# Rotary part of a hybrid decoder layer: two head tiles share one inverse root, the rotation moves to VectorE

## The chip, the cores and the metric

The kernel runs on one core of one Trainium2 chip. The metric is the device time of one execution in microseconds, as the median of several runs.

## What is computed

One step of a decoder layer for a prompt of 512 positions and 32 sample positions (8 sequences of 4), 544 columns in all: a SwiGLU block, a mixing block, and a second SwiGLU block. The mixing block projects the normed input to q, k, v of eight attention heads and to q, k, v, o and gates of four mLSTM heads. The change touches the q and k of the attention heads:

```python
h = _rmsnorm(x, p['mix_norm'])
z = h @ w_in
aq = _rope(_rmsnorm(aq.reshape(B, T, N_ATT_HEADS, HEAD_DIM), q_gain), pos)
ak = _rope(_rmsnorm(ak.reshape(B, T, N_ATT_HEADS, HEAD_DIM), k_gain), pos)
...
x1, x2 = xf[..., :half], xf[..., half:]
return jnp.concatenate([x1 * cos - x2 * sin, x1 * sin + x2 * cos], axis=-1)
```

So each head of 64 numbers is divided by the root of its mean square, multiplied by a gain, and rotated by position. The norm of the whole input (`mix_norm`, the factor `rb` below) also ends in a number per column.

## The kernel before

Everything is kept transposed: features lie on the 128 partitions, the 544 columns (`N`) along a row, worked as two halves of 272 (`HN`). A weight matrix is cut into jobs of 128 output rows. `Raw` loads the weights (tile `wraw`), `Job.split` makes a rounded part `whi` on ScalarE and a rest `wlo` on VectorE, and `products` runs 48 matmuls per job (8 blocks of rows, three products, two halves) into a PSUM tile `mm`, of which there are two. The `after` of a job, a generator, empties that tile.

The mixing block's jobs are, in this order: the gates; q0 to q3; k0, k1, v0, v1; the four of mLSTM head 0; k2, k3, v2, v3; the mLSTM heads 1 to 3; then sixteen short jobs of `w_out`. `rope` is the `after` of the q and k jobs: tile j holds heads 2j and 2j+1. It multiplies the product by `rb` (`rz<-mm,rb`), squares it (`rs<-rz`, ScalarE), has SP's DMA queue swap the halves of each head into `rr`, sums the squares with a 128x128 matmul of ones (`aux<-rs,ca`), takes the inverse root in three ScalarE and three VectorE steps (`rsqrt`), rotates on GpSimd (`rz<-rz,cg`, `rr<-rr,sg`, `rz<-rz,rr`), and multiplies both (`rq<-rz,ry`). Tables `cg` and `sg` hold the gains with cosines and sines. `q_done`, `k_done` then transpose the tiles to rows for the outputs; `attention` begins with the products of q and k, `aux<-rq,rq`; `far_scores` multiplies cache rows with q on GpSimd (`pr<-kv,qb`), where q comes back by way of a DRAM tile `q_d`.

What sets the order is a planner inside the program, `Order`: each generator yields the time at which it can go on by the planner's own costs, and instructions are issued in that order. Each engine then runs its own list strictly in order, and SP's DMA queue does too. A change of one generator therefore moves everything after it in the same stage. All recorded instructions carry line 223 (other engines), 282 or 287 (TensorE).

`wo(m, last)` takes the products of `w_out`: eight jobs with the mLSTM heads 0 to 2 (three blocks of rows), then eight with mLSTM head 3 and the four attention tiles (five blocks), in the order 7, 0, 1, 2, 3 of `mixed`.

Of the kernel before, what the change touches and what calls it, by code (L numbers as in the profile page):

```python
# [8 lines left out]
F32 = mybir.dt.float32  # L9
F32R = mybir.dt.float32r  # L10
AF = mybir.ActivationFunctionType
OP = mybir.AluOpType
# [4 lines left out]
P = 128  # L17
D = 1024
S = 512
B = 8  # L20
T = 4
NS = B * T
N = S + NS
HN = N // 2
# [7 lines left out]
HD = 64  # L32
ROW = NH * HD
NM = 4
EPS = 1e-6
# [3 lines left out]
NK = P + T  # L39
# [12 lines left out]
class Order:  # L52
# [26 lines left out]
    def done(self, *tiles, kind="aux"):  # L79
        for p in tiles:  # L80
            self.free[kind].append(self.used[p.tensor.name][0] + 0.2)
# [58 lines left out]
    def R(self, *aps):  # L140
        return max(self.ready.get(a.tensor.name, (0.0, ""))[0] for a in aps) + 0.2
# [103 lines left out]
def hybrid_layer_kernel(ctx: ExitStack, tc: tile.TileContext, I: dict, C: dict, O: list):  # L245
# [8 lines left out]
    dram = ctx.enter_context(tc.tile_pool(name="scratch", bufs=1, space=DRAM))  # L254
    ctx.enter_context(tc.manual_schedule())

    od = Order()
    act, dve, pool = Engine(od, "act", nc.scalar), Engine(od, "dve", nc.vector), Engine(od, "pool", nc.gpsimd)
    dma = Engine(od, "dma", nc.sync)
    dma2 = pool  # L260
    R, U, done = od.R, od.U, od.done

    def halves(ap):
        return ap.rearrange("p (a b) -> p a b", a=2)
# [10 lines left out]
    def t2(name, shape=(P, N), dt=F32):  # L275
        return gp.tile(list(shape), dt, name=name, tag="t2", bufs=NT2)
# [4 lines left out]
    def mm(out, lhsT, rhs, start=True, stop=True, beside=False, **kw):  # L281
        nc.tensor.matmul(out, lhsT, rhs, start=start, stop=stop, **kw)  # L282
        n = size(rhs)
        od.issue("pe", 0.05 if beside else n / (2180.0 if rhs.dtype == F32R else 595.0), [out], [lhsT, rhs])
# [20 lines left out]
    epsc = small("epsc", (P, 1))  # L305
# [177 lines left out]
    def rsqrt(y, v, t):  # L483
        act.activation(t, v, AF.Ln)
        act.activation(y, t, AF.Exp, scale=-0.5)
        act.activation(t, y, AF.Square)
        yield R(t) - 0.3
        dve.tensor_tensor(t, t, v, op=OP.mult)
        dve.tensor_scalar(t, t, -0.5, 1.5, op0=OP.mult, op1=OP.add)
        dve.tensor_tensor(y, y, t, op=OP.mult)  # L490
# [351 lines left out]
    jobs = ffn_jobs("ffn1", lambda: n1, n2.add)  # L842
# [44 lines left out]
    rb = lambda: n2.rb  # L887
# [16 lines left out]
    for i, n in enumerate(("q_norm", "k_norm")):  # L904
        g = I[n]
# [20 lines left out]
    big = {}  # L926

    def masks_in():
        yield 0, 0, lambda: at[0] >= last_fast + 2
        a = wp.tile([P, 8, P], F32, name="ca", tag="wsp", bufs=8).rearrange("p k c -> p (k c)")  # L930
        b = wp.tile([P, 4 * P + NK + 2 * FAR * 32], F32, name="cb", tag="wsp", bufs=8)
        n = 0
        for t, names in ((a, (("maskA", S), ("bmask", 2 * NS), ("caus", P), ("ones64", P))), (b, (("maskR", 4 * P + NK),))):
            n = 0
            for name, w in names:
                big[name] = t[:, n:n + w]
                dma.dma_start(big[name], C[name])
                n += w
        big["sF"] = b[:, n:].rearrange("p (g i b h) -> p g i b h", g=2, i=FAR, b=4)
# [33 lines left out]

    qT, kT, vT, vR = [None] * 4, [None] * 4, [None] * 4, [None] * 4

    def rope(dst, j, i, last):
        def post(ps, full):
            yield 0, 0, lambda: rb() is not None
            z, r, sq = t2("rz"), t2("rr"), t2("rs")
            dve.tensor_tensor(halves(z), ps, halves(rb()), op=OP.mult)  # L980
            done(full, kind="mm")
            yield R(z) - 0.3
            act.activation(sq, z, AF.Square)
            yield R(z)
            for e in range(2):
                dma.dma_start(r[64 * e:64 * e + 32], z[64 * e + 32:64 * e + 64])
                dma.dma_start(r[64 * e + 32:64 * e + 64], z[64 * e:64 * e + 32])
            yield R(sq), 2
            v = t2("rv")
            mss = aux(), aux()  # L990
            for h, ms in enumerate(mss):
                mm(ms[:, :HN], big["ones64"], sq[:, h * HN:(h + 1) * HN])
                act.activation(v[:, h * HN:(h + 1) * HN], ms[:, :HN], AF.Identity, bias=epsc)
            done(*mss)
            yield R(r) - 0.3, 0, lambda: i in tabs
            z2 = t2("rz2")
            pool.tensor_tensor(z2, z, tabs[i][0], op=OP.mult)
            pool.tensor_tensor(r, r, tabs[i][1], op=OP.mult)
            pool.tensor_tensor(z2, z2, r, op=OP.add)
            z = z2  # L1000
            y = t2("ry")
            yield R(v) - 0.5
            yield from rsqrt(y, v, sq)
            yield R(z) - 0.3
            q = t2("rq")
            dve.tensor_tensor(q, z, y, op=OP.mult)
            dst[j] = q
            if j % 2 and last:
                od.spawn(last(j // 2), 2, R(dst[j]))
        return post  # L1010

    def plain(dst, j, last):
        def post(ps, full):
# [666 lines left out]
    def pair_jobs(c0, afters):  # L1680
        r = Raw(w_in, 0, 8, [c0, c0 + P])
        return [Job(r, i, mxs, a) for i, a in enumerate(afters)]

    def q_jobs(g):
        return pair_jobs(256 * g, [rope(qT, 2 * g + i, 0, q_done) for i in range(2)])

    def kv_jobs(g):
        return (pair_jobs(512 + 256 * g, [rope(kT, 2 * g + i, 1, k_done) for i in range(2)])
                + pair_jobs(1024 + 256 * g, [plain(vT, 2 * g + i, v_done) for i in range(2)]))

    def ml_jobs(h):
# [12 lines left out]
    def wo(m, last):  # L1704
        def post(ps, full):
            yield 0, 0, lambda: xT[m] is not None
            x = xT[m]
            dve.tensor_tensor(halves(x), ps, halves(x), op=OP.add)
            done(full, kind="mm")
            if last:  # L1710
                yield from n3.add(m)
            yield 0
        return post
# [2 lines left out]
        r = Raw(w_out, 4 * P, 3, [m * P, (m + 1) * P])  # L1716
        jobs += [Job(r, i, lambda k: mixed[4 + k], wo(m + i, False)) for i in range(2)]
    for m in range(0, KD, 2):
        r = Raw(w_out, 7 * P, 1, [m * P, (m + 1) * P], (0, 4))
        jobs += [Job(r, i, lambda k: mixed[(7, 0, 1, 2, 3)[k]], wo(m + i, True)) for i in range(2)]  # L1720

    yp = y_prompt[0].rearrange("(b p) d -> p b d", p=P)
    ysm = y_sample.flatten_outer_dims()
# [29 lines left out]
def constants():  # L1753
    import numpy as np

    f = np.float32
    c = {"ident": np.eye(P, dtype=f)}
    half = HD // 2
    inv = (10000.0 ** (-np.arange(half) / half)).astype(f)
    pos = np.concatenate([np.arange(S), PAST + np.tile(np.arange(T), B)]).astype(f)  # L1760
    ang = (pos[None, :] * inv[:, None]).astype(f).astype(np.float64)
    cs, sn = np.cos(ang).astype(f), np.sin(ang).astype(f)
    c["cos"] = np.concatenate([cs, cs, cs, cs], 0)
    c["sin"] = np.concatenate([-sn, sn, -sn, sn], 0)
    c["ones64"] = np.kron(np.eye(2), np.full((HD, HD), 1.0 / HD)).astype(f)
    a = np.arange(P)
    c["caus"] = np.where(a[:, None] <= a[None, :], 0.0, NEG).astype(f)
    s = np.arange(NS)
    ok = (s[:, None] // T == s[None, :] // T) & (s[:, None] <= s[None, :])
    c["causS"] = np.where(ok, 0.0, NEG).astype(f)  # L1770
    c["bmask"] = np.broadcast_to((s[None, :] // T % 2 == np.arange(2)[:, None]).astype(f).reshape(1, -1), (P, 2 * NS)).copy()
    mine = a % NS // T // 2 == a // NS
    c["own"] = ((a[:, None] % NS == s[None, :]) & mine[:, None]).astype(f)
    c["bm4"] = np.stack([mine & (a % NS // T % 2 == 0), mine & (a % NS // T % 2 == 1), ~mine], 1).astype(f)

    def bias(d, n):
        return np.where(n > 0, 8.0 * np.log(np.maximum(n, 1)), NEG).astype(f)

    d = 128 * (3 - np.arange(4))[None, :, None] + a[:, None, None] - a[None, None, :]
    n = ((d <= 128).astype(int) + (d % 4 == 0) + (d % 16 == 0)) * (d >= 0)  # L1780
    c["maskA"] = bias(d, n).reshape(P, S)
    c["hmask"] = (a[:, None] % NH == np.arange(NH)[None, :]).astype(f)
    c["sel"] = (a[:, None] // NH == np.arange(16)[None, :]).astype(f)
    i = a[:, None] // T + 32 * np.arange(3)[None, :]
    n2 = 1 + ((512 - 4 * i) % 16 == 0)
    bf = np.concatenate([bias(i, n2), np.zeros((P, 1), f)], 1)
    t = np.arange(T)[None, :]
    d = 128 + t - a[:, None]
    bn = bias(d, (1 + (d % 4 == 0) + (d % 16 == 0)) * (d <= 128))
    tt, uu = np.arange(T)[:, None], np.arange(T)[None, :]  # L1790
    bw = bias(tt, np.where(tt == uu, 3, np.where(uu < tt, 1, 0)))
    rt = a // NH % T
    far = np.where(rt[:, None, None] == a[None, None, :] % T, bf.T[None], NEG)
    c["maskR"] = np.concatenate([far.reshape(P, 4 * P), bn.T[rt], bw[rt]], 1).astype(f)
    c["brow"] = (a[:, None] // 32 == np.concatenate([np.arange(B), np.arange(B) - 4])[None, :]).astype(f)
    return c
# [35 lines left out]
```

## Time and profile before

| what | value |
|---|---|
| median of 3 runs | 1139.76 us (1139.7 to 1139.85) |
| the profiled execution, its own time | 1140.47 us |
| its span, first to last instruction | 1138.7 us |
| TensorE busy | 1110.7 us (98%) |
| VectorE busy | 783.9 us (69%) |
| ScalarE busy | 516.1 us (45%) |
| GpSimd busy | 155.5 us (14%) |
| mean granted TensorE clock | 0.996 |

The rows further down come from one execution, the profiled one, so sums are made against 1140.47 us. A bracket behind a row of a timeline is the time for which the engine was idle before that instruction, and what it waited for. TensorE's instructions overlap in the records: what one costs is read from start to start.

### The profile page before, as it was taken

The numbers are of one execution on the slowest core, as the hardware profiler recorded it, in microseconds if no ns is written. First come the engines' busy times: TensorE is split into PE (matmuls) and PEld (weight loads), VectorE is DVE, ScalarE is ACT, GpSimd is POOL, SyncE is SP. The second block draws the span as 40 slices with busy tenths as digits, with TensorE's granted clock in tenths as the row PEclk, the third lists the DMA queues.
The fourth block names the chain that finished last, engine by engine and source line by source line (L and its number), as shares of the span: only waits on it lengthen the run. The fifth ranks groups of instructions, "written<-read, shape, count | busy, mean of one in ns | idle before, by whom it ended". The sixth has DMA issues, their size and how long they took to land.

```text
span 1138.7 us, 21430 instructions
## 1 busy us (share of the span) xinstructions
PE 1110.7 (98%) x8819; PEld 1057.8 (93%) x8819; DVE 783.9 (69%) x1199; ACT 516.1 (45%) x926; POOL 155.5 (14%) x137
## 2 busy tenths in 40 slices
PE   7999999999999998999999999999999999999998
PEld 5989999999999998988877779999999999999998
DVE  5988337873487689889866546678972588537851
ACT  5545215451245455556653634463551345414541
POOL 0110000000000035467743201001100000000000
PEclk9999999999999998999999999999999999999999
DMA  7214412432143362685788644442233132422232
GB/s 229 75 40 131 132 38 75 141 119 76 37 139 107 115 212 68 191 276 172 239 268 281 205 128 136 126 149 75 75 112 104 28 128 75 149 75 74 66 104 59
DMA packets 141901, 143.12 MB, mean 126 GB/s; under 512 B 8453, under 2 KB 120485, under 8 KB 141805
## 3 DMA queue, kind: packets, MB, share of 16 engines
q1 hardware_dynamic: 141740, 141.76, 39.9%
q8 instruction: 69, 1.13, 0.4%
q14 instruction: 28, 0.22, 0.1%
q0 software_dynamic: 64, 0.00, 0.0%
HBM read 130.36 MB, written 9.15 MB: 123 GB/s over the span
## 4 chain that ended last, share of the span: by engine, by line
PE 79%; DVE 11%; DMA 3%; ACT 3%; issue 3%; POOL 1%; SPq 1%; ACTq 0%; DVEq 0%; POOLq 0%
PE mm L282 65%; PE aux L282 11%; DVE wlo L223 3%; PE aux L287 3%; ACT whi L223 2%; DMA kv<-in_cache_k_win_dram 2%; DVE ws L223 2%; DVE rs L223 1%; DVE wraw L223 1%; SPq L223 1%; DMA xt<-in_x_prompt_dram 1%; DVE cb L223 1%; DMA wraw<-in_ffn_w_up_dram 1%; DVE mo L223 0%; DVE bcum L223 0%
## 5 line engine op out<-in xcount | busy, mean ns | idle before, releaser
L223 ACT CAST whi<-wraw 128x1024 fp32r<-128x1024 f32 (+3 forms) x180 | 174.0, 986 | 122.7 <-PE mm L282 94.4
L223 DVE TENSOR_TENSOR wlo<-wraw,whi 128x1024 fp32r<-128x1024 f32 (+3 forms) x180 | 209.0, 1170 | 20.8 <-ACT whi L223 20.3
L282 PE MATMUL mm<-oh,wlo 128*128 128x272 f32 x720 | 209.3, 291 | 3.9 <-DVE wlo L223 3.8
L282 PE MATMUL mm<-oh,whi 128*128 128x272 f32 x720 | 207.4, 288 | 0.4 <-ACT whi L223 0.4
L282 PE MATMUL mm<-ol,whi 128*128 128x272 f32 x720 | 207.2, 288 | 0.0
L282 PE MATMUL mm<-xh,whi 128*128 128x272 f32 x720 | 160.7, 305 | 0.2 <-ACT whi L223 0.2
L282 PE MATMUL mm<-xh,wlo 128*128 128x272 f32 x720 | 150.1, 290 | 1.6 <-DVE wlo L223 1.6
L282 PE MATMUL mm<-xl,whi 128*128 128x272 f32 x720 | 150.3, 290 | 0.0
L282 PE MATMUL mm<-hh,whi 128*128 128x272 f32 x704 | 146.2, 289 | 0.0
L282 PE MATMUL mm<-hh,wlo 128*128 128x272 f32 x704 | 145.4, 288 | 0.0
L282 PE MATMUL mm<-hl,whi 128*128 128x272 f32 x704 | 145.4, 288 | 0.0
L223 DVE SCALAR_TENSOR_TENSOR x<-mm,x 128x544 f32<-128x544 f32 x48 | 34.8, 724 | 157.7 <-PE mm L282 157.7
L282 PEld LDWEIGHTS mm<-oh,wlo 128*128 128x128 f32 x720 | 135.4, 188 | 7.1 <-DVE wlo L223 5.9
L282 PEld LDWEIGHTS mm<-oh,whi 128*128 128x128 f32 x720 | 135.5, 188 | 0.7 <-ACT whi L223 0.6
L282 PEld LDWEIGHTS mm<-ol,whi 128*128 128x128 f32 x720 | 135.6, 188 | 0.0
L282 PEld LDWEIGHTS mm<-xh,whi 128*128 128x128 f32 x720 | 113.8, 191 | 12.8 <-issue 10.7
L282 PEld LDWEIGHTS mm<-xh,wlo 128*128 128x128 f32 x720 | 114.2, 190 | 2.0 <-DVE wlo L223 2.0
L282 PEld LDWEIGHTS mm<-xl,whi 128*128 128x128 f32 x720 | 114.3, 190 | 0.1
L282 PEld LDWEIGHTS mm<-hl,whi 128*128 128x128 f32 x704 | 110.4, 188 | 0.0
L282 PEld LDWEIGHTS mm<-hh,wlo 128*128 128x128 f32 x704 | 110.4, 188 | 0.0
L282 PEld LDWEIGHTS mm<-hh,whi 128*128 128x128 f32 x704 | 110.2, 188 | 0.1
L223 ACT CAST whi<-ws 128x1024 fp32r<-128x1024 f32 x54 | 56.7, 1050 | 106.3 <-DVE ws L223 106.2
(322 smaller groups left out, 1870.7 us busy)
## 6 DMA issues: line engine op xcount, KB each, us to landing
wraw<-in_ffn_w_gate_dram SPq DMA_DIRECT2D x40, 512.0 KB
wraw<-in_ffn_w_up_dram SPq DMA_DIRECT2D x36, 512.0 KB
wraw<-in_ffn_w_down_dram SPq DMA_DIRECT2D x16, 1024.0 KB
kv<-in_cache_k_win_dram SPq DMA_DIRECT2D x56, 256.0 KB
kv<-in_cache_v_win_dram SPq DMA_DIRECT2D x56, 256.0 KB
wraw<-in_w_in_dram SPq DMA_DIRECT2D x16, 512.0 KB
wraw<-in_ffn_w_down_dram SPq DMA_DIRECT2D x8, 768.0 KB
wraw<-in_w_in_dram SPq DMA_DIRECT2D x6, 1024.0 KB
```

The costliest lines, as they stand in the source:

```text
L223: r = fn(*args, **kw)
L282: nc.tensor.matmul(out, lhsT, rhs, start=start, stop=stop, **kw)
L287: nc.tensor.transpose(out, in_, idn)
```

## The change

`rope` now serves a pair of tiles. Each half reads the raw product from PSUM twice: ScalarE copies it (`rz`) for the swap and the square, VectorE multiplies it by the cosine table; VectorE also multiplies the swapped copy by the sines and adds. The factor `rb` is no longer multiplied in there. A further generator, `scales`, takes the sums of squares of both tiles with four matmuls whose weights are 32 columns wide, at two column positions, so that the four heads' sums land on rows 0, 1, 32 and 33 of one tile; multiplies them by the square of `rb`; takes one inverse root of 64 rows for both tiles; multiplies by `rb`; writes the four rows to a DRAM tile `y_d` and reads each back onto 64 partitions; and multiplies the rotated tiles by it. The `w_out` jobs take mLSTM head 3 last instead of first.

```diff
+    y_d = dram.tile([4, 4, N], F32, name="y_d")
+    rb2 = []
+
+    def rope(dst, g, i, last):
+        zs, sqs = [None] * 2, [None] * 2
+
+        def scales():
             yield 0, 0, lambda: rb() is not None
-            z, r, sq = t2("rz"), t2("rr"), t2("rs")
-            dve.tensor_tensor(halves(z), ps, halves(rb()), op=OP.mult)
-            done(full, kind="mm")
-            yield R(z) - 0.3
-            act.activation(sq, z, AF.Square)
-            yield R(z)
-            for e in range(2):
-                dma.dma_start(r[64 * e:64 * e + 32], z[64 * e + 32:64 * e + 64])
-                dma.dma_start(r[64 * e + 32:64 * e + 64], z[64 * e:64 * e + 32])
-            yield R(sq), 2
-            v = t2("rv")
+            if not rb2:
+                rb2.append(t2("rb2", (64, N)))
+                act.activation(rb2[0], rb()[0:64], AF.Square)
+            yield R(rb2[0], *sqs) - 0.2, 2
+            v, y, t = t2("rv", (64, N)), t2("ry", (64, N)), t2("rw", (64, N))
             mss = aux(), aux()
             for h, ms in enumerate(mss):
-                mm(ms[:, :HN], big["ones64"], sq[:, h * HN:(h + 1) * HN])
-                act.activation(v[:, h * HN:(h + 1) * HN], ms[:, :HN], AF.Identity, bias=epsc)
+                h_ = slice(h * HN, (h + 1) * HN)
+                for e in range(2):
+                    mm(ms[32 * e:32 * e + 32, :HN], big["ones"], sqs[e][:, h_], beside=e > 0, tile_position=(0, 32 * e))
+                dve.tensor_tensor(v[:, h_], ms[0:64, :HN], rb2[0][:, h_], op=OP.mult)
             done(*mss)
-            yield R(r) - 0.3, 0, lambda: i in tabs
-            z2 = t2("rz2")
-            pool.tensor_tensor(z2, z, tabs[i][0], op=OP.mult)
-            pool.tensor_tensor(r, r, tabs[i][1], op=OP.mult)
-            pool.tensor_tensor(z2, z2, r, op=OP.add)
-            z = z2
-            y = t2("ry")
-            yield R(v) - 0.5
-            yield from rsqrt(y, v, sq)
-            yield R(z) - 0.3
-            q = t2("rq")
-            dve.tensor_tensor(q, z, y, op=OP.mult)
-            dst[j] = q
-            if j % 2 and last:
-                od.spawn(last(j // 2), 2, R(dst[j]))
-        return post
+            yield R(v) - 0.3
+            act.activation(t, v, AF.Ln, bias=epsc[0:64])
+            act.activation(y, t, AF.Exp, scale=-0.5)
+            act.activation(t, y, AF.Square)
+            yield R(y) - 0.3
+            dve.tensor_tensor(y, y, rb()[0:64], op=OP.mult)
+            yield R(t) - 0.3
+            dve.scalar_tensor_tensor(t, v, EPS, t, op0=OP.add, op1=OP.mult)
+            dve.tensor_scalar(t, t, -0.5, 1.5, op0=OP.mult, op1=OP.add)
+            dve.tensor_tensor(y, y, t, op=OP.mult)
+            yield R(y)
+            n = 2 * i + g
+            for e in range(2):
+                dma.dma_start(y_d[n, 2 * e:2 * e + 2], y[32 * e:32 * e + 2])
+            ys = t2("rs"), t2("rs")
+            for e in range(2):
+                for d in range(2):
+                    dma.dma_start(ys[e][64 * d:64 * d + 64], sub(y_d, (4 * n + 2 * e + d) * N, [[0, 64], [1, N]]))
+            for e in range(2):
+                yield R(zs[e], ys[e]) - 0.3
+                q = t2("rq")
+                dve.tensor_tensor(q, zs[e], ys[e], op=OP.mult)
+                dst[2 * g + e] = q
+            od.spawn(last(g), 2, R(*dst[2 * g:2 * g + 2]))
+
+        def half(e):
+            def post(ps, full):
+                yield 0, 0, lambda: i in tabs
+                raw, r, z, sq = t2("rz"), t2("rr"), t2("rz2"), t2("rs")
+                act.copy(halves(raw), ps)
+                dve.tensor_tensor(halves(z), ps, halves(tabs[i][0]), op=OP.mult)
+                done(full, kind="mm")
+                yield R(raw)
+                for d in range(2):
+                    dma.dma_start(r[64 * d:64 * d + 32], raw[64 * d + 32:64 * d + 64])
+                    dma.dma_start(r[64 * d + 32:64 * d + 64], raw[64 * d:64 * d + 32])
+                act.activation(sq, raw, AF.Square)
+                sqs[e] = sq
+                if e:
+                    od.spawn(scales(), 0)
+                yield R(r, z) - 0.3
+                dve.tensor_tensor(r, r, tabs[i][1], op=OP.mult)
+                dve.tensor_tensor(z, z, r, op=OP.add)
+                zs[e] = z
+            return post
...
-        r = Raw(w_out, 7 * P, 1, [m * P, (m + 1) * P], (0, 4))
-        jobs += [Job(r, i, lambda k: mixed[(7, 0, 1, 2, 3)[k]], wo(m + i, True)) for i in range(2)]
+        r = Raw(w_out, 0, 4, [m * P, (m + 1) * P], (7 * P, 1))
+        jobs += [Job(r, i, lambda k: mixed[(0, 1, 2, 3, 7)[k]], wo(m + i, True)) for i in range(2)]
```

The constant `ones64` (128x128) becomes `ones` (128x32, two columns of 1/64 on one head's rows each), and `q_jobs`, `kv_jobs` call `rope` once per pair.

Three places where the lists of instructions move. VectorE before, around the step of the gates that forms `u`; the rows ahead of it are the inverse root of one q tile (`rs`, `ry`), the first reading of the next product (`rz<-mm,rb`) and the rest part of a weight job (`wlo`):

```order
L223 TENSOR_TENSOR wlo<-wraw,whi 128x1024
L223 TENSOR_TENSOR rs<-rs,rv 128x544
L223 TENSOR_SCALAR rs<-rs 128x544
L223 TENSOR_TENSOR ry<-ry,rs 128x544
L223 TENSOR_TENSOR rz<-mm,rb 128x544
L223 TENSOR_TENSOR wlo<-wraw,whi 128x1024
L223 TENSOR_TENSOR u<-bcum,mrow 4x544
```

VectorE of the change at the same step; `rv` is the sums of squares times the square of `rb`, and `rz_4870<-mm,cg` the first reading of a product:

```order
L223 TENSOR_TENSOR wlo<-wraw,whi 128x1024
L223 TENSOR_TENSOR rv<-aux,rb_4632 64x272 x2
L223 TENSOR_TENSOR rz_4870<-mm,cg 128x544
L223 TENSOR_TENSOR wlo<-wraw,whi 128x1024
L223 TENSOR_TENSOR u<-bcum,mrow 4x544
```

The three steps of an inverse root no longer stand between the split of weights and the reading of the product there.

VectorE of the change behind the sums of squares of k0 and k1 (first row), down to the first maxima of the attention (`pS,smax`):

```order
L223 TENSOR_TENSOR rv<-aux,rb_4632 64x272 x2
L223 TENSOR_TENSOR rr<-rr,sg 128x544
L223 TENSOR_TENSOR rz_4870<-rz_4870,rr 128x544
L223 TENSOR_TENSOR wlo<-wraw,whi 128x1024
L223 TENSOR_TENSOR ry<-ry,rb 64x544
L223 TENSOR_TENSOR rr<-rr,sg 128x544
L223 TENSOR_TENSOR rz_4952<-rz_4952,rr 128x544
L223 SCALAR_TENSOR_TENSOR rw<-rv,rw 64x544
L223 TENSOR_SCALAR rw<-rw 64x544
L223 TENSOR_TENSOR ry<-ry,rw 64x544
...
L223 TENSOR_TENSOR rq<-rz_4870,rs 128x544
L223 TENSOR_TENSOR rq<-rz_4952,rs 128x544
```

Ten steps lead to the row `ry<-ry,rw` that goes to DRAM; the two last rows need what comes back (left out between them: v1's reading, two weight splits, the two `rq` of q2 and q3, three steps of mLSTM head 0). Before, each tile's `rq` followed its own root directly.

SP's queue of the change at the same place:

```order
L223 DMA q_d<-qs 32x256
L223 DMA wraw<-in_w_in_dram 128x8x256
L223 DMA y_d<-ry 2x544 x2
L223 DMA rs<-y_d 64x544 x4
L223 DMA out_dram<-vr 128x256 x2
L223 DMA q_d<-qs 32x256
```

Before, the queue held no `y_d` and no `rs<-y_d`; six of them per pair are new, and what follows waits behind them. On TensorE the sums of squares of k0 and k1 stand 126 weight-job matmuls ahead of the first `aux<-rq,rq`, and those of k2 and k3 144 ahead of the transposes of the next mLSTM k tile, whose VectorE reading stands behind the `rq` of k3.

## Rows read from the trace of the kernel before

**Rows 1.** The page, part 1: busy time, share of the span, instructions

```profile
PE 1110.7 (98%) x8819; PEld 1057.8 (93%) x8819; DVE 783.9 (69%) x1199; ACT 516.1 (45%) x926; POOL 155.5 (14%) x137
```

**Rows 2.** Waits of TensorE: who waited for whom, us in total, times, longest

```profile
PE aux L282 <- ACT rs L223: 3.4, 1, 3.4
PE aux L282 <- ACT hN L223: 1.7, 1, 1.7
...
PE aux L287 <- DVE rq L223: 1.0, 1, 1.0
PE aux L287 <- DVE smax L223: 1.0, 1, 1.0
PE mm L282 <- DVE ml L223: 1.0, 1, 1.0
```

**Rows 3.** Timeline of TensorE from 438 to 458: start, duration, instruction, idle before

```profile
440.69 1.08 PE L282 MATMUL aux<-rs,ca 128*128 128x272 f32 x4
441.40 0.61 PE L282 MATMUL mm<-xh,whi 128*128 128x272 f32 x2
441.85 0.41 PE L282 MATMUL mm<-xl,whi 128*128 128x272 f32 x2
...
448.94 2.18 PE L282 MATMUL aux<-rs,ca 128*128 128x272 f32 x4 [3.41 <-ACT rs L223]
450.53 1.04 PE L282 MATMUL mm<-xh,whi 128*128 128x272 f32 x2
...
454.54 0.41 PE L282 MATMUL mm<-xh,wlo 128*128 128x272 f32 x2
```

**Rows 4.** Timeline of VectorE, 427 to 460

```profile
433.67 0.69 DVE L223 TENSOR_TENSOR rs<-rs,rv 128x544 f32<-128x544 f32 x1
434.39 0.44 DVE L223 TENSOR_SCALAR rs<-rs 128x544 f32<-128x544 f32 x1
...
440.59 3.69 DVE L223 TENSOR_TENSOR rs<-rs,rv 128x544 f32<-128x544 f32 x1
444.31 1.48 DVE L223 TENSOR_SCALAR rs<-rs 128x544 f32<-128x544 f32 x1
445.83 1.73 DVE L223 TENSOR_TENSOR ry<-ry,rs 128x544 f32<-128x544 f32 x1
447.48 0.71 DVE L223 TENSOR_TENSOR rz<-mm,rb 128x544 f32<-128x544 f32 x1
```

**Rows 5.** Timeline of GpSimd, 427 to 460

```profile
441.02 1.36 POOL L223 TENSOR_TENSOR rz<-rz,cg 128x544 f32<-128x544 f32 x1
442.34 1.35 POOL L223 TENSOR_TENSOR rr<-rr,sg 128x544 f32<-128x544 f32 x1
```

**Rows 6.** Windows: PE, PEld, DVE, ACT, POOL busy (instructions), granted clock, DMA share, GB/s

```profile
200.00:300.00 100.00, 100.00 (x798) 99.77 (x797) 60.44 (x73) 35.95 (x51) 0.00 (x0) 1.00 0.33 106
...
450.00:452.00 2.00, 2.00 (x8) 1.76 (x7) 2.00 (x2) 1.33 (x3) 2.00 (x2) 0.50 0.00 0
```

**Rows 7.** Timeline of TensorE, 645.8 to 648: four side by side, at 32 columns each

```profile
646.42 1.06 PE L282 MATMUL aux<-kv,pTA 128*32 128x512 f32 x8
647.42 0.44 PE L282 MATMUL aux<-pT,vr 128*64 128x128 f32 x4
```

**Rows 8.** Timeline of VectorE, 456 to 545

```profile
538.42 1.81 DVE L223 TENSOR_TENSOR rs<-rs,rv 128x544 f32<-128x544 f32 x1
540.27 2.38 DVE L223 TENSOR_SCALAR rs<-rs 128x544 f32<-128x544 f32 x1
```

**Rows 9.** Timeline of VectorE, 400 to 420: a PSUM reading of one half

```profile
407.70 0.44 DVE L223 SCALAR_TENSOR_TENSOR nt<-aux,nt 128x272 f32<-128x272 f32 x1
```

**Rows 10.** Timelines of SP's queue, 465 to 473, and of GpSimd, 460 to 480

```profile
466.71 0.52 SPq L223 DMA_DIRECT2D q_d<-qs  x1
467.28 0.41 SPq L223 DMA_DIRECT2D kv<-in_cache_k_win_dram  x1
471.80 0.62 SPq L223 DMA_DIRECT2D qb<-q_d  x1
...
475.10 3.78 POOL L223 TENSOR_TENSOR pr<-kv,qb 128x512 f32<-128x512 f32 x3 [10.06 <-DMA qb<-q_d]
```

**Rows 11.** Tile uw_d: duration min/median/max in ns, first and last start

```profile
L223 SPq DMA_DIRECT2D E<-uw_d x4: 332/376/848, 488.8 to 676.4; - x4
...
L223 SPq DMA_DIRECT2D uw_d<-u x1: 267/267/267, 451.6 to 451.6; - x1
```

More of the change, by code (lines that the diff above doesn't have):

```diff
@@ L932, in masks_in @@
         n = 0
-        for t, names in ((a, (("maskA", S), ("bmask", 2 * NS), ("caus", P), ("ones64", P))), (b, (("maskR", 4 * P + NK),))):
+        for t, names in ((a, (("maskA", S), ("bmask", 2 * NS), ("caus", P), ("ones", NS))), (b, (("maskR", 4 * P + NK),))):
             n = 0
@@ L974, in hybrid_layer_kernel @@
     qT, kT, vT, vR = [None] * 4, [None] * 4, [None] * 4, [None] * 4
-    def rope(dst, j, i, last):
-        def post(ps, full):
-            yield 0, 0, lambda: rb() is not None
-            z, r, sq = t2("rz"), t2("rr"), t2("rs")
-            dve.tensor_tensor(halves(z), ps, halves(rb()), op=OP.mult)
-            done(full, kind="mm")
-            yield R(z) - 0.3
-            act.activation(sq, z, AF.Square)
-            yield R(z)
-            for e in range(2):
-                dma.dma_start(r[64 * e:64 * e + 32], z[64 * e + 32:64 * e + 64])
-                dma.dma_start(r[64 * e + 32:64 * e + 64], z[64 * e:64 * e + 32])
-            yield R(sq), 2
-            v = t2("rv")
+    y_d = dram.tile([4, 4, N], F32, name="y_d")
@@ L1012, in plain @@
+        return [half(e) for e in range(2)]
     def plain(dst, j, last):
@@ L1684, in q_jobs @@
     def q_jobs(g):
-        return pair_jobs(256 * g, [rope(qT, 2 * g + i, 0, q_done) for i in range(2)])
+        return pair_jobs(256 * g, rope(qT, g, 0, q_done))
     def kv_jobs(g):
-        return (pair_jobs(512 + 256 * g, [rope(kT, 2 * g + i, 1, k_done) for i in range(2)])
+        return (pair_jobs(512 + 256 * g, rope(kT, g, 1, k_done))
                 + pair_jobs(1024 + 256 * g, [plain(vT, 2 * g + i, v_done) for i in range(2)]))
@@ L1764, in constants @@
     c["sin"] = np.concatenate([-sn, sn, -sn, sn], 0)
-    c["ones64"] = np.kron(np.eye(2), np.full((HD, HD), 1.0 / HD)).astype(f)
+    c["ones"] = np.pad(np.kron(np.eye(2), np.full((HD, 1), 1.0 / HD)), ((0, 0), (0, NS - 2))).astype(f)
     a = np.arange(P)
```

## The prediction

> **What bounds the kernel now.** I read the page's busy table first: TensorE is at work for 98% of the span [rows 1], so time can only come from work taken off TensorE or from its waits. The waits of TensorE, second, show which of them lie in the mixing stage, the only stage that the change reorders: 3.4 us for the squares of a rope tile, 1.7 for a mLSTM step, 1.0 for a finished k tile, 1.0 for a maximum of the attention, 1.0 for the last mLSTM head [rows 2], 8.1 us together. Third, TensorE's timeline around the longest [rows 3]: it stops for 3.41 us and starts again at 448.94. From there the granted clock is 0.50 [rows 6], the lower of the two levels (1.2 instead of 2.4 GHz), after a stop in which TensorE did nothing. The price is in the starts. A weight-job matmul takes 100/798 = 0.125 us at the full clock [rows 6], a pair 0.25. From 448.94 to 454.54 there are one group of ones-matmuls and 8 pairs: 5.60 us. At the full clock the group costs 441.85 - 440.69 - 0.25 = 0.91 us [rows 3], the 8 pairs 2.0. So the clock costs 5.60 - 2.91 = 2.7 us more, and this one stop 6.1 us.
>
> Fourth, why the squares were late. They need `rz<-mm,rb`, which VectorE began only at 447.48 [rows 4]. Three steps of the tile before stood ahead of it: 3.69, 1.48 and 1.73 us, where the same forms take 0.69, 0.44 and about 0.7 in a quiet stretch (the 0.69 and 0.44 are the first two rows of rows 4, the last is as the first). The quiet ones ran with GpSimd idle; the slow ones lie over GpSimd's rotation of a rope tile [rows 4, 5]. The excess is 5.1 us. So one engine off the path, GpSimd, held VectorE, VectorE held ScalarE, and ScalarE held TensorE.
>
> **The change part by part.** *Sums of squares.* Before: 8 tiles at 0.91 = 7.3 us of TensorE. After: 4 groups of four matmuls, two column positions at once. The lower bound on a group is two streams of 272 columns that share the array fully, 0.91; the upper is no sharing, 1.83. The nearest row is the four streams of 512 at 32 columns each, which take 1.00 from start to next start [rows 7], about the time of one such stream (0.455 x 512/272 = 0.86) with 0.14 for getting in and out. I take 2 x 0.455 + 0.14, and a little for the second way back: 1.1 us. Four groups cost 4.4, so 2.9 us of TensorE time go, all on the path. The Trainium skill (TensorEngine Tiling (Array Packing), Key Properties) says that a change of tiling mode drains TensorE, which speaks against eight such changes, and gives no price; its Theoretical Speedup table would allow twofold, a group of 0.91 and a saving of 3.7. The row's 1.00 instead of 0.86 agrees with a small drain, so I stay with 2.9.
>
> *Rotation off GpSimd.* 24 GpSimd instructions of at least 1.35 us [rows 5] go. GpSimd waits for other data in this stage in any case, once for 10 us [rows 10], so that is worth nothing by itself; it is worth what it held up. The 6.1 us stop goes: the reading of the next product no longer stands behind an inverse root there, and nothing on GpSimd overlaps. The 1.0 for the k tile and the 1.0 for the maximum stood behind the inverse root of k3, whose first two steps took 1.81 and 2.38 us under GpSimd [rows 8], 3.1 more than in quiet: these 2.0 us go too. The 1.7 and the last 1.0 belong to mLSTM heads and are kept.
>
> *VectorE's load.* Per tile it loses the scaling 0.71, 0.69 + 0.44 + 0.7 of the root and the product 0.7: 3.2 us. It gains a reading 0.71, two rotation steps and the product at 0.7, 2.8, and per pair two readings of half a tile at 0.44 [rows 9] and a root of 3 x 0.7 + 0.44: 3.4, half of it per tile. So +1.3 us a tile, +10 in all, beside TensorE. What hides it is the 6.0 us (48 x 0.125) of a job: a q or k job asks 4.5 + 1.2 (a weight split) = 5.7 us, to which the steps of the gates come. Summed in order from the first gate step at 409 to v1's reading, VectorE trails the end of the jobs by up to 2 us, against the 6 us until the PSUM tile is wanted again. If that cover went, the next job would stop for the rest. ScalarE loses about 1 us a tile: nothing.
>
> *DMAs.* Each pair adds two writes at about 0.27 and four reads at about 0.38 [rows 11] to SP: 2.1 us of issue, 8 for four pairs, and SP stops between them until the write has landed. Behind it stand swaps of the next tile, cache rows and weights. Weights are wanted two jobs (12 us) later, which covers that; `far_scores` starts later, and the order leaves its end some 200 weight-job matmuls ahead of the last jobs. The price of the way through DRAM is in the rows of `q_d`: written until 467.23, read back no earlier than 471.80, so 4.6 us; the reader started at 475.10, 2.7 us after the read was issued [rows 10]. So 0.5 + 4.6 + 1.5 + 2.7 = 9.3 us from root to use, where before there was none. The Trainium skill (DMA: Bandwidth & Descriptors, Anatomy of one DMA) puts the fixed part of a DMA at about 2.0 us, most of it the receipt; by that the way would take about 6.0, and the new waits below would vanish, 2.0 us less. The trace's 4.6 differs, and I go by the trace.
>
> *What is late next.* Place one: the first scores of the attention. From the sums of squares of k0 and k1 VectorE has 0.9 + 1.4 + 1.2 + 0.7 + 1.4 + 0.7 + 0.44 + 0.7 = 7.4 us of steps; with the group of 1.1, 9.3 through DRAM and the product 0.7 the first tile is ready after 18.5 us. TensorE has 1.1 + 126 x 0.125 = 16.9 us of work in between, plus transposes that I leave uncounted. So the wait is between 0 and 1.6. Place two: k2 and k3, whose products VectorE makes ahead of reading the next mLSTM k tile. There GpSimd multiplies cache rows all the time, so the steps can take up to 5 us more (as in the stretch of rows 8, four steps in place of 2.6): 23.5 and two products, against 1.1 + 18.0 us plus attention work of a few us. Wait between 0 and 4.4. Both together 0 to 6; I take 2.0, as the transposes and attention work left uncounted make both waits shorter.
>
> *Order of `w_out`.* mLSTM head 3 is used 24 matmuls (3.0 us) later; in the new order its transposes also stand 24 matmuls later. The 1.0 us wait stays: nothing. The attention pairs move later by up to 200 matmuls and still end 84 ahead of their use: nothing.
>
> **The sum**, against the profiled execution: 1140.47 - 2.9 - 6.1 - 2.0 + 2.0 = 1131.5 us. The median of the runs lies 0.7 below that execution, so 1130.8 for the median; with 0 to 6 for the new waits 1128.8 to 1134.8.
>
> **The rivals.** *Waits move, none go.* A new order finds new collisions of about the same size; only the 2.9 us of work go: 1140.47 - 2.9 - 0.7 = 1136.9, give or take 2. For it: VectorE is as full as before, and the stage holds a dozen chains planned to within a microsecond. Against it: the longest wait has a cause that is gone. *All waits go*, new ones don't come: 8.1 + 2.7 less as well, 1126.1. For it, GpSimd has little left to collide with; against it, the mLSTM waits have nothing to do with rope. *The way through DRAM decides, slower.* SP and VectorE run in order, so a late `y_d` blocks VectorE at `rq` and, behind it, the reading of PSUM tiles and weight splits. If TensorE then stops for as long as in rows 3 the clock falls with it, 6.1 us a pair. It decides from the point where the way through DRAM takes some 3.4 us more than the cover, that is from 13 instead of 9.3 us at place one. At two pairs it gives 1140.47 - 11.0 + 12.2 - 0.7 = 1141.0, at three 1147.1, at four 1153.2. For it, the measured 4.6; against it, q2 and q3 have far more cover than k. *The side-by-side matmuls don't overlap*: a group costs 1.83, nothing is saved there, 1133.7; rows 7 speak against it.
>
> **How the numbers follow.** A measurement of this kernel can tell some 0.2%, 2.3 us, from no change. Forecast 0.45, waits move 0.25, all go 0.10, slower through DRAM 0.15, no overlap 0.05. Faster by over 0.2% is below 1137.5: nearly all of the forecast (0.44), half of the second (0.12), 0.10 and 0.05: 0.71. Slower by over 0.2% is the third rival: 0.14. The rest, 0.15, is within. The range goes from 1125.5, under the case without waits, to 1141.5, where the DRAM case begins to bite.
>
> **What would show it.** Right: TensorE's wait for rope squares at about 445 gone and the granted clock 1.00 from 436 to 460; about 1.1 us for each of four groups `aux<-rs,ca` at 32 columns; no GpSimd on rope; VectorE's root steps at 0.4 to 0.7 us in the q jobs; SP waiting about 4 us for `y_d` per pair; a wait of TensorE of some 2 us for `rq` or behind it. Wrong: a stop of over 3 us with the clock at 0.50 after it; `y_d` landing in 2 us or in 8; waits elsewhere in the mixing stage that add up to 8 us again.

## The result and the profile after

The changed kernel takes **1130.34 us** (median of 4 runs, 1128.79 to 1133.5) beside 1139.73 for the kernel before (4 runs): a ratio of 0.9922, 95% interval 0.9901 to 0.9943. The forecast was 1130.8. Two later sets of 6 runs each gave 1131.62 and 1130.38. The profiled execution is the longest of its four: 1133.5 us, span 1131.7.

The busy table of the page [rows 1 before]:

```profile
PE 1106.0 (98%) x8819; PEld 1054.1 (93%) x8819; DVE 771.3 (68%) x1222; ACT 504.4 (45%) x900; POOL 112.0 (10%) x113
```

GpSimd is busy 43.5 us less, 42.0 of it the rotation. VectorE has 23 instructions more and is busy 12.6 us less.

To tell the mixing stage from the noise of the rest I measure it in each trace between two marks of TensorE that every version has: the squares of the norm ahead of it and of the norm behind it. The two marks in the timeline of the kernel before:

```profile
404.30 1.08 PE L282 MATMUL aux<-sq,onesd 128*128 128x272 f32 x4
...
756.65 1.08 PE L282 MATMUL aux<-sq,onesd 128*128 128x272 f32 x4
```

and of the changed kernel:

```profile
405.83 1.08 PE L282 MATMUL aux<-sq,onesd 128*128 128x272 f32 x4
...
749.70 1.08 PE L282 MATMUL aux<-sq,onesd 128*128 128x272 f32 x4
```

The stage went from 352.35 to 343.87 us, 8.5 less. The first mark alone moved by 1.5 us, in a part of the program that the change doesn't touch; so spans of single executions carry a noise of that size, and stages are better compared.

Waits of TensorE in the stage, 400 to 760, of the changed kernel (who waited for whom; total, times, longest) [rows 2 before]:

```profile
PE aux L287 <- DVE mk L223: 2.9, 1, 2.9
PE aux L282 <- ACT kt L223: 1.5, 2, 1.2
PE aux L287 <- DMA kv<-in_cache_k_win_dram: 1.0, 1, 1.0
PE aux L287 <- DVE C L223: 0.8, 1, 0.8
PE aux L282 <- DVE Cst L223: 0.3, 1, 0.3
```

Not one wait of before is left but that for a cache row (0.2 us before), and not one of the new ones is for rope. The stretch in which TensorE stopped before runs without a gap at the full clock (windows: busy, granted clock, DMA share) [rows 3, 6 before]:

```profile
445.00:450.00 5.00, 5.00 (x42) 1.00 0.76 221
450.00:455.00 5.00, 5.00 (x50) 1.00 0.38 111
```

The longest new wait, 2.9 us for an mLSTM k tile, looks like the old one: slowed steps of VectorE ahead of the one that TensorE wants. VectorE's timeline ahead of it:

```profile
590.77 1.77 DVE L223 TENSOR_TENSOR mo<-mo,ms 128x544 f32<-128x544 f32 x1
592.58 1.69 DVE L223 SCALAR_TENSOR_TENSOR mo<-mo,ms 128x544 f32<-128x544 f32 x1
594.19 1.86 DVE L223 TENSOR_REDUCE cb<-pr 128x8 f32<-128x512 f32 x3
595.97 0.71 DVE L223 SCALAR_TENSOR_TENSOR mk<-mm,rb 128x544 f32<-128x544 f32 x1
```

and GpSimd's, which multiplies cache rows for the sample scores at that moment:

```profile
590.67 3.02 POOL L223 TENSOR_TENSOR pr<-kv,qb 128x512 f32<-128x512 f32 x2 [1.26 <-ACT sqj L223]
594.04 1.35 POOL L223 TENSOR_TENSOR pr<-kv,qb 128x512 f32<-128x512 f32 x1 [0.35 <-PE aux L282]
```

Two products of an output gate take 1.77 and 1.69 us, where a product of that form takes 0.71 with GpSimd idle (`rr<-rr,sg` at 434.95 in this trace), and `mk`, which TensorE wants, is behind them. Their excess is 2.0 of the 2.9 us; no run takes GpSimd's products away there, so this cause is read from the rows and not tested. The page SBUF — State Buffer of the Trainium skill (Who interferes with whom) says that a VectorE step with two SBUF inputs contends with a GpSimd step that reads SBUF, and that the pair of ports they share is an exclusive lock. These rows and [rows 4, 5] agree: there the step that VectorE starts at 440.59 ends at 444.28, 0.6 us behind the end of GpSimd's second step (442.34 + 1.35 = 443.69), which is about its quick time of 0.69.

### The profile page after: what moved, and what is told of

Same layout as the page of the kernel before. It is cut to its first block, busy times and chain, and to the rows that moved or that the text cites. A ratio compares the mean times of both kernels' runs of the same rounds, so it can differ in the third digit from the quotient of the medians.

```text
span 1131.7 us, 21405 instructions
## 1 busy us (share of the span) xinstructions
PE 1106.0 (98%) x8819; PEld 1054.1 (93%) x8819; DVE 771.3 (68%) x1222; ACT 504.4 (45%) x900; POOL 112.0 (10%) x113
## 5 line engine op out<-in xcount | busy, mean ns | idle before, releaser
L282 PEld LDWEIGHTS mm<-xh,whi 128*128 128x128 f32 x720 | 113.3, 191 | 12.6 <-issue 11.4
```

## The experiments

A caution for all of them: a planner orders this stage, so each edit that adds or moves a step changes the order of much else. What is read from a run is its own waits, not its total alone. `stage` is the time between the two marks in the profiled execution.

| run | edit | median us (runs) | stage us |
|---|---|---|---|
| before | | 1139.73 (4) | 352.35 |
| changed kernel | | 1130.34 (4) | 343.87 |
| again, a third time | none | 1131.62 (6), 1130.38 (6) | 343.22, 341.17 |
| e1 | before + new `w_out` order | 1138.4 (10) | 352.5 |
| e2 | before + rotation on VectorE | 1134.7 (5) | 348.9 |
| e3, twice | changed, rotation on GpSimd | 1135.91 (10), 1135.14 (6) | 343.66, 348.04 |
| e5 | changed, old `w_out` order | 1135.19 (5) | 348.4 |
| e6 | changed, twice through DRAM | 1134.39 (4) | 348.4 |
| v1b | changed, `mk` 3 us later | 1131.88 (4) | 343.0 |
| v2, twice | changed, `mk` and `mv` 3 us later | 1129.39 (4), 1127.92 (6) | 339.3, 341.68 |
| v4 | changed, `mk` 3, `mv` 2 us later | 1131.31 (4) | 343.44 |

### Rotation alone off GpSimd

```diff
-            pool.tensor_tensor(z2, z, tabs[i][0], op=OP.mult)
-            pool.tensor_tensor(r, r, tabs[i][1], op=OP.mult)
-            pool.tensor_tensor(z2, z2, r, op=OP.add)
+            dve.tensor_tensor(z2, z, tabs[i][0], op=OP.mult)
+            dve.tensor_tensor(r, r, tabs[i][1], op=OP.mult)
+            dve.tensor_tensor(z2, z2, r, op=OP.add)
```

> The kernel before with the three rotation steps on VectorE instead of GpSimd; the four-row sums, the way through DRAM and the new w_out order are not in it. Theory (GpSimd's rotation under VectorE's inverse root causes the stop of TensorE at 445): the stop of 3.4 us and its 2.7 us of clock go, and the root steps take 0.4 to 0.7 us; 1133.7 us (1131 to 1137, since VectorE gets 2.1 us more a tile). Rival (the gain comes from the new reading and summing of the tiles, not from GpSimd): 1139.7, a stop of over 2 us remains for the rope squares.

Measured: 1134.7 us, ratio 0.9956 (0.994 to 0.9972), as the theory said. The reading of the next product stands behind the root as before, but the root's steps in VectorE's timeline are quick, and the reading follows at once:

```profile
441.43 0.72 DVE L223 TENSOR_TENSOR rs<-rs,rv 128x544 f32<-128x544 f32 x1
442.18 0.44 DVE L223 TENSOR_SCALAR rs<-rs 128x544 f32<-128x544 f32 x1
442.66 0.73 DVE L223 TENSOR_TENSOR ry<-ry,rs 128x544 f32<-128x544 f32 x1
443.30 0.72 DVE L223 TENSOR_TENSOR rz<-mm,rb 128x544 f32<-128x544 f32 x1
```

No stop for the rope squares is left. This part alone bought 5.0 us. Its new order also brought stops elsewhere, one of 4.0 us (waits of TensorE):

```profile
PE aux L287 <- DVE mv L223: 4.0, 1, 4.0
PE aux L287 <- ACT vs L223: 2.0, 1, 2.0
```

The longer one is not GpSimd's: ahead of `mv` VectorE stood idle for 4.16 us, which the trace puts down to an outgoing transfer of `kr`.

### Rotation back on GpSimd in the new scheme

```diff
-                dve.tensor_tensor(r, r, tabs[i][1], op=OP.mult)
-                dve.tensor_tensor(z, z, r, op=OP.add)
+                pool.tensor_tensor(r, r, tabs[i][1], op=OP.mult)
+                pool.tensor_tensor(z, z, r, op=OP.add)
```

> The changed kernel with the product with the sines and the sum put back on GpSimd, two of the three rotation steps that were there. Theory (GpSimd's work slows VectorE's steps that lie over it): VectorE's root steps in the q jobs go from 0.4-0.7 us to 1 to 3.7 us, rope products come later, +2 to +6 us: 1132.5 to 1136.5. Rival (the rotation on GpSimd is harmless once the reading of PSUM tiles no longer stands behind the root): 1128.8 to 1131.5, as the changed kernel.

> The changed kernel with two rotation steps on GpSimd a second time, for a profile of a slower execution: the ten runs so far went from 1130.9 at a clock of 0.999 to 1139.6 at 0.992. Theory: a stop of TensorE of 1.5 us or more (for smax or ml) is followed by a low clock in the slow executions and not in the quick one; 1133 to 1139, stage 346 to 352 us. Rival: the slow executions have longer waits at the rope tiles, with rope steps on VectorE of over 1 us.

The median fits the theory (+4.8 us over the median 1131.1 of all 16 runs of the changed kernel), its mechanism does not; with the rival it is the other way round. The root's last three steps in the q jobs stay at 0.4 to 0.7 us (one step ahead of them, `ry<-ry,rb` at 442.49, takes 1.24), TensorE has no gap from 407 to 455, and the profiled execution of the first set is as quick as the changed kernel. In the second profile two `rq` from 443.95 take 3.68 us under GpSimd's rotation, with the reading of the next product behind them, and TensorE still has no gap there. So where GpSimd's rotation slows VectorE in this order, the delay fits into the room that the order leaves. What costs the time is seen by putting the two profiles, a quick execution and a slower one, side by side. Timeline of TensorE and windows (busy, granted clock, DMA share) of the first:

```profile
683.52 0.52 PE L282 MATMUL mm<-ml,whi 128*128 128x272 f32 x2 [1.49 <-DVE ml L223]
```

```profile
510.00:520.00 10.00, 8.38 (x61) 1.00 0.82 234
570.00:580.00 10.00, 8.31 (x68) 1.00 0.98 308
680.00:690.00 10.00, 7.68 (x58) 1.00 0.06 19
```

and of the second:

```profile
685.24 0.52 PE L282 MATMUL mm<-ml,whi 128*128 128x272 f32 x2 [1.49 <-DVE ml L223]
```

```profile
510.00:520.00 10.00, 7.83 (x47) 0.83 0.82 239
570.00:580.00 10.00, 8.25 (x61) 0.89 1.04 336
680.00:690.00 10.00, 7.68 (x40) 0.85 0.06 23
```

The waits are nearly the same (for `ml` 1.49 us in both, for `smax` 1.6 and 2.2, for a cache row 1.6 and 1.8); in the one execution the clock stays at 1.00 behind each, in the other it falls behind these three. The theory of the second run holds, its rival falls: the two executions of one program differ by 4.4 us of stage. Longer waits are 0.7 of it, and the three windows lose (0.17 + 0.11 + 0.15) x 10 = 4.3 us of clock, somewhat more than the 3.7 that are left. That the same makes the median of e3 higher rests on these two executions alone.

### The order of `w_out`

```diff
-        r = Raw(w_out, 7 * P, 1, [m * P, (m + 1) * P], (0, 4))
-        jobs += [Job(r, i, lambda k: mixed[(7, 0, 1, 2, 3)[k]], wo(m + i, True)) for i in range(2)]
+        r = Raw(w_out, 0, 4, [m * P, (m + 1) * P], (7 * P, 1))
+        jobs += [Job(r, i, lambda k: mixed[(0, 1, 2, 3, 7)[k]], wo(m + i, True)) for i in range(2)]
```

This is e1, on the kernel before; e5 is the reverse on the changed kernel.

> The kernel before with the new order of w_out alone. My prediction put this part at nothing. Theory: only the 1.0 us wait for the last mLSTM head goes, about 1138.8 us (1138.2 to 1139.8). Rival, the new order of w_out carries a good part of the gain by itself: below 1136.

> The changed kernel with the old order of w_out (the last mLSTM head first again). Theory: the head is wanted 24 matmuls (3.0 us) earlier than it is now, so a wait of 1 to 3 us comes back there, with some of the clock: 1131.5 to 1136. Rival (the order is worth nothing, as I predicted): 1128.8 to 1131.5.

e1: 1138.4 us, ratio 0.9992 (0.9978 to 1.0006), so no difference that the runs can tell; its rival falls. The wait for `ml` is gone, but two waits for cache rows grew by 0.9 us together, and the stage is as long as before. e5: 1135.19 us, 4.1 over the 16 runs, as its theory said. The head's wait is back and longer, and the head's transposes (`aux<-ident,hN`) stand directly ahead of its first use (timeline of TensorE, and windows around it):

```profile
712.90 0.60 PE L287 MATMUL aux<-ident,hN 128*128 128x128 f32 x4
...
715.89 0.52 PE L282 MATMUL mm<-mh,whi 128*128 128x272 f32 x2 [2.03 <-ACT mh L223]
```

```profile
710.00:720.00 10.00, 7.73 (x50) 0.88 0.35 111
720.00:730.00 10.00, 10.00 (x78) 0.95 0.19 56
```

2.3 us of stop and (0.12 + 0.05) x 10 = 1.7 of clock make the 4. In the kernel before, 24 weight-job matmuls stand between the same transposes and the head's first use, and only the rest part of the head, `ml`, is waited for:

```profile
716.88 0.60 PE L287 MATMUL aux<-ident,hN 128*128 128x128 f32 x4
...
722.17 0.51 PE L282 MATMUL mm<-ml,whi 128*128 128x272 f32 x2 [0.97 <-DVE ml L223]
```

So the order is worth nothing that can be measured in the kernel before and 4 us in the changed one, where the planner, left with the old order, puts no weight-job matmul between the head's transposes and its use.

### Twice through DRAM

```diff
+            yt = t2("ry2", (4, N))
+            dma.dma_start(yt, y_d[n])
+            dma.dma_start(y_d2[n], yt)
-                    dma.dma_start(ys[e][64 * d:64 * d + 64], sub(y_d, (4 * n + 2 * e + d) * N, [[0, 64], [1, N]]))
+                    dma.dma_start(ys[e][64 * d:64 * d + 64], sub(y_d2, (4 * n + 2 * e + d) * N, [[0, 64], [1, N]]))
```

> The changed kernel with the root sent through DRAM twice per pair (written, read back to a small tile, written again, then spread). It tells how much room the way through DRAM has. Theory (the way takes about 6 us from root to product, 2.4 us of it the last landing, and the order has room for it): each pair's rows come 4 to 6 us later, total 0 to +3 us against the changed kernel, 1129 to 1133. Rival (the DRAM way is at the edge, as my slower case had it): a stop with its clock at two or more pairs, +6 us a pair, 1142 or more.

Measured: 1134.39 us, 2.8 over the changed kernel beside it: inside the forecast difference of 0 to 3, though 1.4 above the 1133 that was to be its upper end. SP's queue for the first pair, in the changed kernel:

```profile
437.13 0.70 SPq L223 DMA_DIRECT2D y_d<-ry  x2
438.59 2.42 SPq L223 DMA_DIRECT2D rs<-y_d  x4
```

and with the second trip:

```profile
435.73 0.69 SPq L223 DMA_DIRECT2D y_d<-ry  x2
437.46 0.24 SPq L223 DMA_DIRECT2D ry<-y_d  x1
440.52 0.24 SPq L223 DMA_DIRECT2D y_d<-ry  x1
441.97 2.42 SPq L223 DMA_DIRECT2D rs<-y_d  x4
```

The last reads start 6.2 instead of 1.5 us after the first write, 4.8 us later per pair, and neither `rq` nor the rope squares stop TensorE. Its longest stop is 2.4 us for an mLSTM tile, and the longest with a rope name in it, 1.2 for `rv`, precedes the trip. So the order had room for these 4.8 us at each pair, and the rival falls. Where the 2.8 us go was not traced; no wait of TensorE names the trip.

### Moving the mLSTM tiles from the edge

```diff
-            yield R(k), 1, on("gates")
+            yield R(k) + 3.0, 1, on("gates")
```

and in v2 and v4 the same for the v tile, `R(vt)`, with 3.0 and 2.0.

> The changed kernel once more, with more runs, as the thing to compare the others with, and for a second profile. Theory: the executions differ by whether the clock falls after TensorE's stop of about 2.9 us at 594; where it does not fall, 1128.5 to 1130, where it does, some 3 us more. Rival: the stop or other waits themselves change length between executions, with the clock at 1.00 everywhere.

> The changed kernel with the transposes of an mLSTM k tile placed 3 us later in the planned order, so that TensorE has other work while VectorE is late with that tile. Theory: the stop of 2.9 us at 594 and the clock after it go, and nothing else gets as late: 1126 to 1129. Rival (a new order finds new collisions of about the same size): 1129 to 1136.

> As the run before, with the transposes of the mLSTM v tiles 3 us later too. Theory: no stop of over 1.5 us in the mixing stage, clock 1.00 from 407 to 755, 1126 to 1129. Rival: new collisions, 1129 to 1136.

> The changed kernel a third time, beside the run that follows, so that the two have the same chip. By ten runs so far 1128.8 to 1133.5, median about 1131.6; the mixing stage (from the squares of the norm ahead of it to those behind it) 343 to 344 us in a profile.

> The kernel with the transposes of the mLSTM k and v tiles 3 us later, once more with more runs. Theory: it is really faster than the changed kernel, by 2 to 4 us: median 1127.5 to 1129.7, mixing stage 339 to 340 us in the profile. Rival: its four runs were lucky, and its median is within 1 us of the changed kernel's beside it.

> As the run before, with the k transposes 3 us and the v transposes 2 us later. Theory (moving a tile off its edge is a gain of its own): mixing stage 339 to 341 us, 1127.5 to 1130. Rival (each order that the planner finds has its own collisions, and the gain of the run before is one of several draws): stage 342 to 347 us, 1130.5 to 1135.

The changed kernel again: the clock fell less behind the `mk` stop in the second profile and not at all in the third, and their times are 1129.89 and 1127.73 us against 1133.5 in the first. That fits the theory in the main (1127.73 lies below the 1128.5 forecast for no fall); the other waits differ too, by up to 1.4 us in sum. v1b: the `mk` stop is gone, waits of 1.7, 1.5 and 1.4 us for other tiles came, no gain. v2: 2.2 and 2.5 us below the changed kernel in two sets; its ratios to before, 0.9905 (0.9886 to 0.9925) and 0.9897 (0.988 to 0.9914), overlap with those beside them, 0.9927 (0.9912 to 0.9942) and 0.9918 (0.9901 to 0.9934). It is probably the best version here, and not by its mechanism: the theory wanted no stop over 1.5 us, and the two profiles have one of 2.2 and one of 3.1; the second one's stage, 341.68, is also longer than the 339 to 340 forecast. v4, a microsecond away, gives nothing: 1131.31 and a stage of 343.44, both as its rival said. That speaks for the rival, by which every new order is a draw; it does not show it.

## Why the prediction was right, step by step

**The stop at 445, minus 6.1: the idle part shown, the clock part not fixed.** The 3.41 us of idle went, in e2 too, where the rotation alone left GpSimd; so the chain GpSimd, VectorE, ScalarE, TensorE, named in the prediction, was the cause. Of the 2.7 us for the clock three profiles of the changed kernel tell more. Each has the same 2.89 us wait for `mk`. The first:

```profile
596.83 1.08 PE L287 MATMUL aux<-ident,mk 128*128 128x128 f32 x4 [2.89 <-DVE mk L223]
...
604.23 1.06 PE L282 MATMUL aux<-kv,pTA 128*32 128x512 f32 x8
```

the second:

```profile
594.50 0.63 PE L287 MATMUL aux<-ident,mk 128*128 128x128 f32 x4 [2.89 <-DVE mk L223]
...
600.76 1.07 PE L282 MATMUL aux<-kv,pTA 128*32 128x512 f32 x8
```

the third:

```profile
593.26 0.63 PE L287 MATMUL aux<-ident,mk 128*128 128x128 f32 x4 [2.89 <-DVE mk L223]
...
597.96 1.27 PE L282 MATMUL aux<-kv,pTA 128*32 128x512 f32 x8
```

From the restart to the same later instruction it takes 7.40, 6.26 and 4.70 us. The third ran at 1.00 throughout (its window 590 to 600), so a stop of 2.9 us was followed by 2.7, 1.6 or no us of lost clock. I had read the 2.7 of one execution as a fixed price. It is one value of several, here the largest.

**Ones-matmuls, minus 2.9: somewhat too much.** The group of the second pair in the changed kernel, timeline of TensorE:

```profile
436.30 0.41 PE L282 MATMUL mm<-xh,wlo 128*128 128x272 f32 x2
436.64 1.11 PE L282 MATMUL aux<-rs,ca 128*32 128x272 f32 x8
437.68 0.52 PE L282 MATMUL mm<-xh,whi 128*128 128x272 f32 x2
438.03 0.42 PE L282 MATMUL mm<-xl,whi 128*128 128x272 f32 x2
```

438.03 - 436.30 - 2 x 0.25 = 1.23 us, against 1.1 forecast: about 0.1 is lost ahead of the group and 0.1 behind, where weight jobs start 0.34 and 0.35 apart instead of 0.25. Four groups save 7.3 - 4.9 = 2.4 us. The rival without overlap (1.83) is refuted.

**The other waits, minus 2.0 and plus 2.0: right in sum, wrong in both places.** Gone are not only `rq` and `smax` (2.0), but also the two that I kept, `hN` 1.7 and `ml` 1.0, a cache row's 0.2, and a stop that I had not seen at all. It lies inside a group of the kernel before, where the view of waits shows nothing:

```profile
593.08 3.08 PE L282 MATMUL aux<-kv,pTA 128*32 128x512 f32 x8
```

The same eight matmuls take 1.06 in [rows 7]: 2.0 us more. In e1 the same group lasts 3.08 as well, and there the trace names a late value row of the cache for 0.58 of idle ahead of it; that this was the cause in both is likely, not shown. So 6.9 us went and 6.5 came (7.0 and 5.6 in the other profiles), none of it for the root that comes back from DRAM. "Waits move" was the right rival for this part: the experiments on the changed kernel and e2 show 3.6 to 9.1 us of them in their profiles.

**The way through DRAM, 9.3 us: 5.3 measured.** The failed step is the landing of the write. I read it from `q_d`, written until 467.23 and read from 471.80, as 4.6 us [rows 10], and SP's waits of before do put 4.1 us of that down to `q_d`. But it does not carry over to `y_d`. SP's waits in the changed kernel, 400 to 560:

```profile
SPq L223 <- DMA y_d<-ry: 2.8, 4, 0.7
```

0.7 a pair. `q_d` is 32 KB and was written while the DMA engines were busy to 0.70 (466 to 472); `y_d` is 4.2 KB a write, at 0.28 to 0.45. Which of the two makes the difference no run here separates; in the changed kernel `q_d` itself, at 0.70 again, no longer makes SP wait (written from 469.93, read from 473.18). So 4.6 us is not even a fixed price of `q_d`. By the signs that I had set, `y_d` landing within 2 us is one for wrong, and the wait of some 2 us for `rq` did not come. The whole trip is seen in e3, where VectorE waits for it; in the three profiles of the changed kernel it never does. SP's queue and VectorE's timeline there:

```profile
457.28 0.53 SPq L223 DMA_DIRECT2D y_d<-ry  x2
458.55 2.40 SPq L223 DMA_DIRECT2D rs<-y_d  x4
```

```profile
456.54 0.72 DVE L223 TENSOR_TENSOR ry<-ry,rw 64x544 f32<-64x544 f32 x1
462.54 1.94 DVE L223 TENSOR_TENSOR rq<-rz,rs 128x544 f32<-128x544 f32 x2 [0.56 <-DMA rs<-y_d]
```

From the root's end, 457.26, to the product, 462.54, it is 5.3 us. The other terms were about right: 0.5 for two writes, 1.2 for the two reads of the first tile (all four take 2.40, not 1.5), and 2.8 from their issue (459.75) to use. The landing is not the only reason why the new waits of 2.0 did not come. In the changed kernel the root of k0 and k1 ends at 463.95, and the first `aux<-rq,rq` runs at 474.04. With the transposes that I left uncounted that is 19.5 us behind the sums of squares (454.49) instead of 16.9. By an estimate from these rows even a trip of 9.3 us would just have fitted: 463.95 + 9.3 + 0.7 = 473.95. The Trainium skill (DMA: Bandwidth & Descriptors, Anatomy of one DMA) gives its fixed 2.0 us for DMAs that GpSimd issues, and these are SP's. The estimate worked out from it, about 6.0 for the trip, was still nearer than mine; I set a row of another size of write above it.

**Order of `w_out`, nothing: wrong.** The count was right: 24 weight-job matmuls stand between the head's transposes and its first use before, and 24 after. What I did not ask is where the transposes would stand in the changed kernel without this edit; e5 shows none in between, and 4 us. The wait that I kept went as well, because the way from the transposes to the end of `ml` took 5.2 us before (716.88 to 722.11) and 3.7 after (714.24 to 717.95).

**VectorE's load, +10 and covered: covered, but not +10.** It keeps up in the q jobs; where it is late, at `mk`, GpSimd's cache products lie over its steps. The +10 us set quick times against quick times. In the trace of before the rope steps took 9.9 + 9.7 + 8.6 + 6.6 + 5.7 = 40.5 us, slowed under GpSimd; after the change they take 37.2, near the 8 x 3.2 + 10 = 36 forecast.

**The sum.** For the three profiles: 2.4 + 6.1 + 6.9 less the new waits (6.5, 7.0, 5.6) and the new clock (2.7, 1.6, 0) is 6.2, 6.8 and 9.8 us; the stage lost 8.5, 9.1 and 11.2. From 1.4 to 2.3 us are left open. They are no idle time of TensorE: of its 8.41 us in the stage before (352.35 less 343.94 busy) all but 0.1 is in the named waits, and of its 6.51 after all is. They lie within runs of matmuls, as the 2.0 us above do. The four-row sums were never run without the rest of the change; their 2.4 us are read from rows. The mechanism of the stop was right. That the total came within 0.5 us was luck: the waits that I kept and the one that I missed balanced those, and the clock, that I did not foresee.

## What to carry to other kernels

When two engines off the path slow each other's steps, look for what stands behind the slowed steps in the same queue: the cure is either to move one engine's work or to take the urgent reading out from behind it, and either removed the stop here (e2, e3). In a planned order every edit redraws the small waits, so judge it by the cause that it removes and by a stage between two marks, and expect some microseconds of waits to come back under other names. The landing of one DMA is no price for another of an eighth of its size; where a trip is new, look for more than one row and keep the spread.

## What the runs showed of the hardware that was not expected

- The same stop of the same program was followed by a lower clock in one execution and by none in another: 2.89 us with a loss of 2.7, 1.6 and 0 us; in e3 1.49 us with a clock of 1.00 and of 0.85 in its window. The Trainium skill (TensorE: Matmul & The Clock Gate, What's actually happening) says that the chip's watch on activity is not started by the kernel; by that one program can meet the clock differently from one execution to the next, and the three profiles agree with it. No run tests it.
- Four matmuls on two column positions cost 1.23 us, 0.3 more than the 0.91 of the two matmuls of before; about 0.1 of it lies ahead of the group and 0.1 behind.
- Writes of 4.2 KB to DRAM by SP let a read of the same rows start 1.3 to 1.5 us after the first issue (437.13 to 438.59, 457.28 to 458.55), where 32 KB had taken 5.1 (466.71 to 471.80).
